# Attention scores of head pairs: plain rounded parts on 64 rows each instead of stacked parts on 128

## The chip, the cores and the metric

One core of a Trainium2 chip runs the whole network in one launch. The metric is device time in microseconds (us), the median of several executions.

## The reference, cut to what matters

Four layers work on x of 512 tokens by 1024 channels in float32. Layers 0 and 3 mix with differential attention (A), layer 1 with latent attention (B), layer 2 with dilated attention (C); each is followed by a SwiGLU block. What the change touches are the scores of A and of the undilated group of C, whose heads are all 64 channels wide:

```python
# A, layers 0 and 3: 8 pairs of heads; a pair shares its values
q = apply_rope(q, cos, sin) * 64 ** -0.5
k = apply_rope(k, cos, sin)
p = softmax(einsum('bhqd,bhkd->bhqk', q, k))          # 16 heads, 512 x 512 each
a = p[:, :, 0] - lam * p[:, :, 1]                     # the two heads of a pair
o = rms_norm(a @ v, subln) * (1.0 - lambda_init)
# C, layer 2: 16 heads, three groups (window, dilation); group 0 is (128, 1)
q = apply_rope(q, cos, sin) * 64 ** -0.5
s = where(abs(qpos - kpos) <= 64, q @ k.T, -1e30)     # group 0: a band of keys
```

## The kernel before, in words

Every float32 product that needs accuracy is made of numbers rounded to the fast matmul type: x = hi + lo, where ACT rounds (`act` with an F32R output) and DVE or POOL subtracts (`tt` with `subtract`). A projection is three products into one PSUM bank: hi·hi, hi·lo, lo·hi (`mm3`, `project`, lines 604 to 614).

The program is first written down as a list of operations with an estimated cost, an engine, and the buffers that they read and write (`Plan.op`). `Plan.run` (line 401) then schedules that list several times with changing priorities, keeps the plan with the shortest estimate, and issues the instructions in that plan's order. So the order on every engine hangs on the estimated costs of all operations; each operation stays whole, and its matmuls follow one another. PSUM has 8 banks. Buffers come from rings: a new tile waits until the tile that had its slot is no longer used.

**A** (`layer_a`, line 998). For each of 8 head pairs `rope` (line 1017) projects 128 channels of q, then of k; the upper and the lower 64 partitions of the result belong to the two heads of the pair. DVE multiplies by the cosine table and shuffles, POOL multiplies by the sine table and adds. The tables `cs` were multiplied at the start by 1/rms of each token (line 1012). `qk` (line 1046) splits: for each head s, tile `qa[s]` holds the rounded q in the head's own 64 partitions and the rest of q in the other 64; `ka[s]` holds the rounded k twice; `kl` holds the rest of k. That is 6 ACT and 4 POOL instructions on 64 partitions for each pair, in 5 tiles of a ring of 10.

For each of the 4 query tiles (line 1068) a score tile is one operation of four matmuls with 512 columns (line 1073): for each head one product over all 128 rows of the array (hi·hi and lo·hi together, as the parts are stacked), then for each head one product on its 64 rows (hi·lo). Each head's scores fill a bank, out of a ring of four. Then DVE takes the negative maximum of each head (`negmax`, line 1076), scales the two maxima by 1/8 (`ts`, line 1078, which appears at L354 in the profile), ACT takes the exponentials with scale 1/8, that bias and a row sum (line 1082), DVE inverts each of the two sums (`recip`, lines 1085 and 1087, L364), combines, and PE turns the result with four transposes (L293). The probabilities live in a ring of 5 tiles.

**C** (`layer_c`, line 1350). For each of 8 head pairs and each of three groups, `rope` (line 1372) makes q and k. For group 0 `split` (line 1384) does what `qk` does, out of a ring of 5. The scores of two query tiles, each against 256 keys, are one operation of eight matmuls (lines 1457 to 1467): for each query tile two on 128 rows, then two on 64 rows. Groups 1 and 2 multiply unsplit float32 q and k, head by head on 64 rows (line 1473): four query tiles of 128 keys in one operation. The later products with the values use all rows and half the columns of the array (`halves`, line 265, L271).

All matmuls of `mm` appear at L261, activations at L317, `tt` at L330, `stt` at L341, `negmax` at L368, the shuffle at L385.

Of the kernel before, what the change touches and what calls it, by code (L numbers as in the profile page):

```python
# [7 lines left out]
F32 = mybir.dt.float32  # L8
# [6 lines left out]
T = 512  # L15
# [163 lines left out]
class Plan:  # L179
# [85 lines left out]
    def halves(self, *parts):  # L265

        nc = self.nc

        def fn():
            for out, l, r, s, e in parts:  # L270
                nc.tensor.matmul(out.ap(), l.ap(), r.ap(), start=s, stop=e)  # L271

        cost = sum(p[2].n / 0.6 + 60.0 for p in parts[::2])
        return self.op("pe", cost, fn, _uniq([v for p in parts for v in p[1:3]]), _uniq([p[0] for p in parts]), lag=340.0)

    def tiled(self, *parts):
# [236 lines left out]
def _uniq(views):  # L513
    out, seen = [], set()
    for v in views:
        k = (id(v.buf), v.p0, v.p1, tuple(v.free))
        if k not in seen:
            seen.add(k)
            out.append(v)
    return out  # L520
# [26 lines left out]
class Net:  # L547
# [450 lines left out]
    def layer_a(self, i, j):  # L998
# [4 lines left out]
        pr, sr, tr = (Ring(p, b) for b in (self.bank[0:2], self.bank[2:6], self.bank[6:8]))  # L1003
        small = list(self.small)
        take = lambda n: Ring(p, [small.pop(0) for _ in range(n)])
        o_ring, v_ring, qk_ring, p_ring = take(16), take(8), take(10), take(5)
        aT_h, aT_l = Ring(p, self.big[0:1]), Ring(p, self.big[1:2])
        self.tables("c_rope_a")
        r = self.norm(tr)
        cs = self.rt  # L1010
        for c in range(2):
            p.tt(cs[:, c, :], cs[:, c, :], self.rb.all, ALU.mult)
        swap = [(d + 8) % 16 if d < 16 else d for d in range(32)]
        sub = self.kept.new([128, 1])
        p.ts(sub.all, self.gcol(self.rows["a_subln"] + j), 1.0 - init, ALU.mult)
# [1 line left out]
        def rope(c0):  # L1017
            ps = self.project(pr, self.wblock(w, 0, KT, c0, 128), KT, self.xk)
            q, t = self.tmp.new([128, T]), self.tmp.new([128, T])
            p.tt(q.all, ps.all, cs[:, 0, :], ALU.mult)  # L1020
            p.shuffle(t.all, ps.all, swap)
            p.tt(t.all, t.all, cs[:, 1, :], ALU.mult, eng="pool")
            p.tt(q.all, q.all, t.all, ALU.add, eng="pool")
            return q
# [20 lines left out]

        def qk(h):

            q = rope(128 * h)
            qa = [qk_ring.new([128, T], F32R) for _ in range(2)]
            for s, (a, b) in enumerate(HALVES):  # L1050
                p.act(qa[s][a, :], q[a, :])
                p.tt(qa[s][b, :], q[a, :], qa[s][a, :].bits(F32), ALU.subtract, eng="pool")
            k = rope(D + 128 * h)
            ka = [qk_ring.new([128, T], F32R) for _ in range(2)]
            kl = qk_ring.new([128, T], F32R)
            for s, (a, b) in enumerate(HALVES):
                p.act(ka[s][a, :], k[a, :])
                p.act(ka[s][b, :], k[a, :])
                p.tt(kl[a, :], k[a, :], ka[s][a, :].bits(F32), ALU.subtract, eng="pool")
            return qa, ka, kl  # L1060

        oh = []
        nxt = qk(0)
        for h in range(A_HEADS):
            qa, ka, kl = nxt
            th, tl = aT_h.new([128, NT, T], F32R), aT_l.new([128, NT, T], F32R)
            l0 = self.cols2.new([128, NT])
            for t in range(NT):
                st = self.cols.new([128, 6])
                es = [self.psum(sr) for _ in range(2)]  # L1070
                tq = slice(128 * t, 128 * (t + 1))

                p.mm(*[(es[s].all, qa[s][:, tq], ka[s].all, True, False) for s in range(2)],
                     *[(es[s].all, qa[s][HALVES[s][0], tq], kl[HALVES[s][0], :], False, True) for s in range(2)])
                for s in range(2):
                    p.negmax(st[:, s:s + 1], es[s].all)
                sc = self.cols.new([128, 2])
                p.ts(sc.all, st[:, 0:2], A_HD ** -0.5, ALU.mult)
                pe = []
                for s in range(2):  # L1080
                    e = p_ring.new([128, T])
                    p.act(e.all, es[s].all, ACTF.Exp, scale=A_HD ** -0.5, bias=sc[:, s:s + 1], accum=st[:, 2 + s:3 + s])
                    pe.append(e)

                p.recip(l0[:, t:t + 1], st[:, 2:3])
                rl = self.cols.new([128, 1])
                p.recip(rl.all, st[:, 3:4])
                p.stt(rl.all, rl.all, self.lam[:, j:j + 1], st[:, 2:3], ALU.mult, ALU.mult)
                a = pe[0]
                p.stt(a.all, pe[1].all, rl.all, pe[0].all, ALU.mult, ALU.add)  # L1090
                ps = self.psum(tr, (128, NT, 128))
                p.transposes(*[(ps[:, c, :], a[:, 128 * c:128 * (c + 1)], self.ident.all) for c in range(NT)])
                b = slice(128 * t, 128 * (t + 1))
                p.act(th[:, :, b], ps.all)
                p.tt(tl[:, :, b], ps.all, th[:, :, b].bits(F32), ALU.subtract)
            if h + 1 < A_HEADS:
                nxt = qk(h + 1)
            if h % 2 == 0:
                vv = values(h // 2)
            ps = self.psum(tr)  # L1100
            hd = slice(128 * (h % 2), 128 * (h % 2) + 128)
            for c in range(NT):
                self.mm3(ps.all, vv[0][c // 2][:, c % 2, hd], vv[1][c // 2][:, c % 2, hd], th[:, c, :], tl[:, c, :], c == 0, c == NT - 1)
            o, sq = self.tmp.new([128, T]), self.tmp.new([128, T])
            p.act(o.all, ps.all)
            p.act(sq.all, ps.all, ACTF.Square)
            s = self.colsum(tr, self.tokens(sq, False))
            v = self.cols.new([128, NT])
            p.tt(v.all, s, l0.all, ALU.mult)
            p.tt(v.all, v.all, l0.all, ALU.mult)  # L1110
            p.ts(v.all, v.all, 0.5 / A_HD, ALU.mult, EPS, ALU.add)
            ro = self.rpow(v.all, NT)
            p.tt(ro.all, ro.all, l0.all, ALU.mult)
            bc = self.spread(tr, ro)
            p.stt(o.all, o.all, sub.all, bc.all, ALU.mult, ALU.mult)
            hh, hl = o_ring.new([128, T], F32R), o_ring.new([128, T], F32R)
            p.act(hh.all, o.all)
            p.tt(hl.all, o.all, hh.all.bits(F32), ALU.subtract)
            oh.append((hh.all, hl.all))
# [230 lines left out]
    def layer_c(self, i, j):  # L1350
# [30 lines left out]
                p.tt(tiles(q.all), perm(a.all), perm(t.all), ALU.add)  # L1381
            return q

        def split(q, k):

            new = lambda: f_ring.new([128, T], F32R)
            qa, ka, kl = [new(), new()], [new(), new()], new()
            for s, (a, b) in enumerate(HALVES):
                p.act(qa[s][a, :], q[a, :])
                p.tt(qa[s][b, :], q[a, :], qa[s][a, :].bits(F32), ALU.subtract, eng="pool")  # L1390
                p.act(ka[s][a, :], k[a, :])
                p.act(ka[s][b, :], k[a, :])
                p.tt(kl[a, :], k[a, :], ka[s][a, :].bits(F32), ALU.subtract, eng="pool")
            return qa, ka, kl

        def values(g, v):

# [40 lines left out]
        for n in range(C_HEADS // 2):  # L1438
            P = {}
            sn, sp = st_ring.new([128, G, NT, 4]), st_ring.new([128, G, NT, 4])  # L1440
            for g in range(G):
                q, k = rope(3 * D * g + 128 * n, g), rope(3 * D * g + D + 128 * n, g)
                st = sn if g == 0 else sp
                if g == 0:
                    qa, ka, kl = split(q, k)

                hb = (slice(0, 64), slice(64, 128))
                if g == 0:
                    for t0 in (0, 2):
                        ps = [self.psum(sr, (128, 2, 256)) for _ in range(2)]  # L1450
                        e = 0 if t0 == 0 else 448
                        mms, spans = [], ([], [])
                        for h in range(2):
                            P[g, h, t0] = pieces[0]
                            pieces.append(pieces.pop(0))
                            p.memset(P[g, h, t0](e, e + 64), 0.0)
                        for t in (t0, t0 + 1):

                            lo = min(max(0, 128 * t - 64), T - 256)
                            d = lo - (128 * t - 64)  # L1460
                            c = slice(max(0, d), min(256, 256 + d))
                            tk, ks, o = slice(128 * t, 128 * (t + 1)), slice(lo, lo + 256), 256 * (t - t0)
                            mms += [(ps[h][:, t - t0, :], qa[h][:, tk], ka[h][:, ks], True, False) for h in range(2)]
                            mms += [(ps[h][:, t - t0, :], qa[h][hb[h], tk], kl[hb[h], ks], False, True) for h in range(2)]
                            for h in range(2):
                                spans[h].append((t, ps[h][:, t - t0, c.start - d:c.stop - d], c, P[g, h, t0](o + c.start, o + c.stop)))
                        p.mm(*mms)
                        for h in range(2):
                            self.exps(spans[h], st, g, h, scale)
                else:  # L1470
# [162 lines left out]
```

## Time and profile before

| what | us |
|---|---|
| median of 3 executions (2767.26 to 2769.59) | 2769.24 |
| the profiled execution | 2773.31 |
| its span, first to last instruction | 2771.5 |
| PE busy in the span | 2728.5 |
| DVE / ACT / POOL busy in the span | 2016.8 / 1442.2 / 699.9 |
| mean granted TensorE clock, share of full | 0.994 |

The profile shows one execution with every instruction's start and duration. PE are matmuls, PEld the weight loads that precede them and run beside the matmul before. A matmul's recorded duration has a modelled end and overlaps the next one, so what one costs is read from start to start. In the shapes, `64*128` is an array use of 64 rows and 128 columns, `128x512` the moving operand; a row that ends in x8 merges eight instructions.

### The profile page before, as it was taken

How to read it: one execution, taken by the hardware profiler on the slowest of the kernel's cores; microseconds unless marked ns; L12 is line 12 of the kernel's file. 1: busy time of each engine (PE TensorE's matmuls, PEld its weight loads, DVE VectorE, ACT ScalarE, POOL GpSimd, SP SyncE). 2: the span in 40 equal slices, each digit the busy share in tenths (PEclk: the TensorE clock that was granted, in tenths of full speed). 3: DMA queues.
4: the chain of work that ended last, by engine and by line, in shares of the span. 5: the costliest groups of instructions: out<-in, count | busy, mean ns of one | idle time of the engine just before them, and what ended most of it. 6: DMA issues, size and time to landing. Idle time of an engine off the chain costs nothing.

```text
span 2771.5 us, 43850 instructions
## 1 busy us (share of the span) xinstructions
PE 2728.5 (98%) x16565; PEld 2330.3 (84%) x16565; DVE 2016.8 (73%) x3727; ACT 1442.2 (52%) x2673; POOL 699.9 (25%) x510
## 2 busy tenths in 40 slices
PE   8999999999999999999999999999999999999999
PEld 6777899997777899988888888789998777789998
DVE  6786888766665887765758575688776688688774
ACT  5564544445874544445555555454444566454442
POOL 3343211003642210021413222221002444221101
PEclk9999999999999999999999999999999999999999
DMA  5211343323122343232222322333323211324322
GB/s 142 61 46 54 103 126 100 111 77 72 35 62 80 88 118 104 84 109 78 70 78 70 85 67 80 96 88 116 106 81 110 61 46 55 94 81 121 101 79 66
DMA packets 474977, 235.80 MB, mean 85 GB/s; under 512 B 47935, under 2 KB 471694, under 8 KB 474766
## 3 DMA queue, kind: packets, MB, share of 16 engines
q1 hardware_dynamic: 474766, 233.00, 29.8%
q8 instruction: 130, 2.13, 0.3%
q14 instruction: 81, 0.66, 0.1%
HBM read 230.66 MB, written 2.29 MB: 84 GB/s over the span
## 4 chain that ended last, share of the span: by engine, by line
PE 93%; DVE 3%; ACT 1%; DMA 1%; issue 1%; POOL 0%; SPq 0%; POOLq 0%; DVEq 0%; ACTq 0%
PE b L261 87%; PE b L293 4%; PE b L271 2%; ACT s L317 1%; DVE s L330 0%; DVE col L368 0%; PE b L282 0%; POOL tmp L330 0%; DVE wlo L330 0%; DVE tmp L330 0%; DVE tmp L385 0%; DVE s L341 0%; DMA raw<-in_a_w_qkv 0%; DVE tmp L341 0%; DVE raw L330 0%
## 5 line engine op out<-in xcount | busy, mean ns | idle before, releaser
L261 PE MATMUL b<-s,whi 128*128 128x256 f32 (+1 forms) x4000 | 867.0, 312 | 3.6 <-ACT s L317 1.4
L261 PEld LDWEIGHTS b<-s,whi 128*128 128x128 f32 x4000 | 654.7, 188 | 63.5 <-DVE tmp L330 2.3
L261 PE MATMUL b<-s,wlo 128*128 128x256 f32 (+1 forms) x2000 | 622.5, 311 | 0.8 <-DVE wlo L330 0.8
L317 ACT ACTIVATE whi<-raw 128x1024 fp32r<-128x1024 f32 (+4 forms) x350 | 367.7, 1055 | 340.6 <-PE b L261 226.2
L330 DVE TENSOR_TENSOR wlo<-raw,whi 128x1024 fp32r<-128x1024 f32 (+2 forms) x330 | 445.4, 1356 | 68.3 <-ACT whi L317 66.2
L261 PE MATMUL b<-xh,whi 128*128 128x512 f32 x1072 | 434.6, 405 | 8.6 <-DVE tmp L385 4.4
L261 PE MATMUL b<-xh,wlo 128*128 128x512 f32 x1072 | 420.6, 392 | 0.0
L261 PE MATMUL b<-xl,whi 128*128 128x512 f32 x1072 | 420.0, 392 | 0.0
L261 PEld LDWEIGHTS b<-s,wlo 128*128 128x128 f32 x2000 | 376.2, 188 | 25.6 <-DVE wlo L330 1.4
L330 DVE TENSOR_TENSOR tmp<-b,tmp 128x256 f32<-128x256 f32 (+1 forms) x297 | 128.2, 432 | 238.9 <-PE b L261 202.7
L317 ACT ACTIVATE tmp<-b 128x256 f32<-128x256 f32 (+2 forms) x301 | 126.6, 430 | 334.7 <-PE b L261 280.3
L261 PEld LDWEIGHTS b<-xh,whi 128*128 128x128 f32 x1072 | 202.4, 189 | 59.7 <-issue 8.7
L261 PEld LDWEIGHTS b<-xh,wlo 128*128 128x128 f32 x1072 | 202.3, 189 | 44.1
L330 POOL TENSOR_TENSOR tmp<-tmp,rt 128x512 f32<-128x512 f32 x83 | 116.5, 1406 | 468.5 <-DVE tmp L385 399.5
L261 PEld LDWEIGHTS b<-xl,whi 128*128 128x128 f32 x1072 | 202.9, 189 | 37.3
L261 PE MATMUL b<-s,g 128*128 128x256 f32 x1728 | 224.8, 281 | 0.0
L261 PEld LDWEIGHTS b<-s,g 128*128 128x128 f32 x1728 | 218.0, 189 | 5.9
L317 ACT ACTIVATE s<-tmp 128x512 fp32r<-128x512 f32 (+3 forms) x232 | 140.5, 613 | 90.8 <-DVE tmp L341 40.0
L330 POOL TENSOR_TENSOR acc<-acc,tmp 128x512 f32<-128x512 f32 (+1 forms) x56 | 92.9, 1659 | 355.6 <-ACT tmp L317 355.1
L261 PE MATMUL b<-xh,s 128*128 128x512 f32 x512 | 177.0, 395 | 0.0
L330 POOL TENSOR_TENSOR raw<-raw 128x512 f32<-128x512 f32 x36 | 56.5, 1569 | 434.4 <-DVE g L330 355.8
L330 POOL TENSOR_TENSOR raw<-rt,rb 128x512 f32<-128x512 f32 x36 | 58.2, 1617 | 388.9 <-DVE wlo L330 354.1
(184 smaller groups left out, 4864.9 us busy)
## 6 DMA issues: line engine op xcount, KB each, us to landing
raw<-in_f_w_gu SPq DMA_DIRECT2D x144, 256.0 KB, 3.4
raw<-in_c_w_qkv SPq DMA_DIRECT2D x72, 512.0 KB, 3.8
s<-in_f_w_out SPq DMA_DIRECT2D x128, 256.0 KB, 2.9
raw<-in_a_w_qkv SPq DMA_DIRECT2D x48, 512.0 KB, 3.7
rt<-in_f_w_gu SPq DMA_DIRECT2D x72, 256.0 KB, 3.4
raw<-in_f_w_gu SPq DMA_DIRECT2D x32, 512.0 KB, 4.8
raw<-in_f_w_out SPq DMA_DIRECT2D x32, 384.0 KB, 3.5
acc<-in_f_w_gu SPq DMA_DIRECT2D x36, 256.0 KB, 3.2
```

Of the source, the lines that this page charges most:

```text
L261: nc.tensor.matmul(out.ap(), l.ap(), r.ap(), start=s, stop=e, skip_group_check=more)
L271: nc.tensor.matmul(out.ap(), l.ap(), r.ap(), start=s, stop=e)
L293: nc.tensor.transpose(out.ap(), i.ap(), idn.ap())
L317: nc.scalar.activation(out.ap(), in_.ap(), func, **k)
L330: o = self.op(eng, cost, lambda: e.tensor_tensor(out=out.ap(), in0=a.ap(), in1=b.ap(), op=alu), [a, b], [out])
```

## The change

A head's q and k keep their own 64 partitions: `hi` is the rounded tile of both heads, `lo` the rest. Both `qk` and `split` now need one ACT and one POOL instruction on 128 partitions for q, and the same for k. A score tile becomes six products on 64 rows, in the order hi·hi of head 0, of head 1, lo·hi of both, hi·lo of both, through a new helper `pairs` with a cost of its own for the planner; in C twelve products for two query tiles. The scale 1/8 of A goes, as its square root, into the tables of q and k alike, so that the scaling of the maxima falls away; the two inversions become one on two columns. In A the ring of q and k tiles goes from 10 to 8, that of the probabilities from 5 to 7.

```diff
+    def pairs(self, *parts):
+        nc = self.nc
+        def fn():
+            for out, l, r, s, e in parts:
+                nc.tensor.matmul(out.ap(), l.ap(), r.ap(), start=s, stop=e)
+        cost = sum(0.4414 * p[2].n + 12.0 for p in parts[::2]) + 200.0
+        return self.op("pe", cost, fn, ...)
...
-        o_ring, v_ring, qk_ring, p_ring = take(16), take(8), take(10), take(5)
+        o_ring, v_ring, qk_ring, p_ring = take(16), take(8), take(8), take(7)
...
-            p.tt(cs[:, c, :], cs[:, c, :], self.rb.all, ALU.mult)
+            p.stt(cs[:, c, :], cs[:, c, :], A_HD ** -0.25, self.rb.all, ALU.mult, ALU.mult)
...
-            q = rope(128 * h)
-            qa = [qk_ring.new([128, T], F32R) for _ in range(2)]
-            for s, (a, b) in enumerate(HALVES):
-                p.act(qa[s][a, :], q[a, :])
-                p.tt(qa[s][b, :], q[a, :], qa[s][a, :].bits(F32), ALU.subtract, eng="pool")
-            k = rope(D + 128 * h)
-            ka = [qk_ring.new([128, T], F32R) for _ in range(2)]
-            kl = qk_ring.new([128, T], F32R)
-            for s, (a, b) in enumerate(HALVES):
-                p.act(ka[s][a, :], k[a, :])
-                p.act(ka[s][b, :], k[a, :])
-                p.tt(kl[a, :], k[a, :], ka[s][a, :].bits(F32), ALU.subtract, eng="pool")
-            return qa, ka, kl
+            out = []
+            for c0 in (0, D):
+                x = rope(c0 + 128 * h)
+                hi, lo = (qk_ring.new([128, T], F32R) for _ in range(2))
+                p.act(hi.all, x.all)
+                p.tt(lo.all, x.all, hi.all.bits(F32), ALU.subtract, eng="pool")
+                out += [hi, lo]
+            return out
...
-                p.mm(*[(es[s].all, qa[s][:, tq], ka[s].all, True, False) for s in range(2)],
-                     *[(es[s].all, qa[s][HALVES[s][0], tq], kl[HALVES[s][0], :], False, True) for s in range(2)])
+                p.pairs(*[(es[s].all, a[HALVES[s][0], tq], b[HALVES[s][0], :], n == 0, n == 2)
+                          for n, (a, b) in enumerate(((qh, kh), (ql, kh), (qh, kl))) for s in range(2)])
                 for s in range(2):
                     p.negmax(st[:, s:s + 1], es[s].all)
-                sc = self.cols.new([128, 2])
-                p.ts(sc.all, st[:, 0:2], A_HD ** -0.5, ALU.mult)
...
-                    p.act(e.all, es[s].all, ACTF.Exp, scale=A_HD ** -0.5, bias=sc[:, s:s + 1], accum=st[:, 2 + s:3 + s])
+                    p.act(e.all, es[s].all, ACTF.Exp, bias=st[:, s:s + 1], accum=st[:, 2 + s:3 + s])
...
-                p.recip(l0[:, t:t + 1], st[:, 2:3])
+                p.recip(ls[:, :, t], st[:, 2:4])
                 rl = self.cols.new([128, 1])
-                p.recip(rl.all, st[:, 3:4])
-                p.stt(rl.all, rl.all, self.lam[:, j:j + 1], st[:, 2:3], ALU.mult, ALU.mult)
+                p.stt(rl.all, ls[:, 1, t:t + 1], self.lam[:, j:j + 1], st[:, 2:3], ALU.mult, ALU.mult)
...
-                            mms += [(ps[h][:, t - t0, :], qa[h][:, tk], ka[h][:, ks], True, False) for h in range(2)]
-                            mms += [(ps[h][:, t - t0, :], qa[h][hb[h], tk], kl[hb[h], ks], False, True) for h in range(2)]
+                            mms += [(ps[h][:, t - t0, :], a[hb[h], tk], b[hb[h], ks], n == 0, n == 2)
+                                    for n, (a, b) in enumerate(((qh, kh), (ql, kh), (qh, kl))) for h in range(2)]
...
-                        p.mm(*mms)
+                        p.pairs(*mms)
```

`split` of C becomes the same loop as in `qk` above, out of its own ring of 5.

## Rows read from the trace of the kernel before

**Rows 1.** The page, parts 1 and 4: busy time by engine; shares of the chain.

```profile
PE 2728.5 (98%) x16565; PEld 2330.3 (84%) x16565; DVE 2016.8 (73%) x3727; ACT 1442.2 (52%) x2673; POOL 699.9 (25%) x510
...
PE 93%; DVE 3%; ACT 1%; DMA 1%; issue 1%; POOL 0%; SPq 0%; POOLq 0%; DVEq 0%; ACTq 0%
```

**Rows 2.** Stretches (start:end, length, busy by engine with counts, clock, DMA): attention A, C, A.

```profile
33.00:256.00 223.00, 214.78 (x1181) 169.08 (x1182) 176.25 (x371) 131.77 (x266) 102.11 (x71) 0.97 0.20 60
...
1236.00:1755.00 519.00, 517.44 (x3143) 430.18 (x3141) 349.53 (x1065) 278.47 (x711) 149.21 (x97) 1.00 0.28 76
...
2145.00:2370.00 225.00, 214.46 (x1179) 168.74 (x1178) 178.22 (x373) 134.51 (x269) 101.53 (x71) 0.97 0.20 59
```

**Rows 3.** Timeline, PE then PEld: the first two score tiles in a row of A.

```profile
47.01 2.14 PE L261 MATMUL b<-s,s 128*128 128x512 f32 x8
49.08 0.39 PE L261 MATMUL b<-whi,xh 128*128 128x256 f32 x1
...
46.90 0.30 PEld L261 LDWEIGHTS b<-s,s 128*128 128x128 f32 x2
47.56 0.18 PEld L261 LDWEIGHTS b<-s,s 64*128 64x128 f32 x2 [0.36 <-POOL tmp L330]
47.99 0.30 PEld L261 LDWEIGHTS b<-s,s 128*128 128x128 f32 x2 [0.24 <-issue]
48.65 0.18 PEld L261 LDWEIGHTS b<-s,s 64*128 64x128 f32 x2 [0.37 <-issue]
```

**Rows 4.** Timeline, PE: one score tile of A by itself, and what stands beside it.

```profile
77.91 0.62 PE L261 MATMUL b<-g,s 128*128 128x512 f32 x2
78.37 1.05 PE L261 MATMUL b<-s,s 128*128 128x512 f32 x4
79.36 0.50 PE L261 MATMUL b<-xh,whi 128*128 128x512 f32 x1
```

**Rows 5.** Timeline, PE: the last two score tiles in a row.

```profile
2354.23 2.15 PE L261 MATMUL b<-s,s 128*128 128x512 f32 x8
```

**Rows 6.** Timeline, PE then PEld: products on 64 rows of a dilated group, C.

```profile
1261.64 1.16 PE L261 MATMUL b<-s,s 64*128 64x128 f32 x16
...
1261.64 0.97 PEld L261 LDWEIGHTS b<-s,s 64*128 64x128 f32 x16 [0.35 <-issue]
1262.73 0.19 PEld L261 LDWEIGHTS b<-xh,whi 128*128 128x128 f32 x1
```

**Rows 7.** Timeline, PE: score blocks of C, after a projection and after half-column products.

```profile
1253.72 1.45 PE L261 MATMUL b<-s,s 128*128 128x256 f32 x8
1255.10 0.50 PE L261 MATMUL b<-xh,whi 128*128 128x512 f32 x1
...
1386.90 1.57 PE L261 MATMUL b<-s,s 128*128 128x256 f32 x8
1388.40 0.39 PE L261 MATMUL b<-whi,xh 128*128 128x256 f32 x1
```

**Rows 8.** Waits of PE in the first A stretch, then in the second.

```profile
PE b L293 <- DVE col L354: 1.9, 2, 1.6
...
PE b L261 <- DVE col L364: 1.3, 1, 1.3
...
PE b L261 <- DVE col L354: 1.1, 1, 1.1
PE b L261 <- DVE col L364: 1.1, 1, 1.1
```

**Rows 9.** Groups by line and shape, whole span: count, busy us, mean ns, idle before.

```profile
L317 ACT ACTIVATE s<-tmp 64x512 fp32r<-64x512 f32 x96 | 60.5, 630 | 34.6 <-POOL tmp L330 32.9
...
L330 POOL TENSOR_TENSOR s<-tmp,s 64x512 fp32r<-64x512 f32 x64 | 93.4, 1459 | 43.4 <-ACT s L317 39.6 <-PE b L293 1.3
...
L354 DVE TENSOR_SCALAR col<-col 128x2 f32<-128x2 f32 x64 | 24.6, 385 | 0.0
...
L364 DVE RECIPROCAL col<-col 128x1 f32<-128x1 f32 x128 | 19.5, 155 | 24.8 <-ACT s L317 24.6
```

More of the change, by code (lines that the diff above doesn't have):

```diff
@@ L273, in halves @@
         cost = sum(p[2].n / 0.6 + 60.0 for p in parts[::2])
+        return self.op("pe", cost, fn, _uniq([v for p in parts for v in p[1:3]]), _uniq([p[0] for p in parts]), lag=340.0)
+    def pairs(self, *parts):
[4 more added lines that the diff above has]
+        cost = sum(0.4414 * p[2].n + 12.0 for p in parts[::2]) + 200.0
         return self.op("pe", cost, fn, _uniq([v for p in parts for v in p[1:3]]), _uniq([p[0] for p in parts]), lag=340.0)
@@ L1064, in layer_a @@
         for h in range(A_HEADS):
-            qa, ka, kl = nxt
+            qh, ql, kh, kl = nxt
             th, tl = aT_h.new([128, NT, T], F32R), aT_l.new([128, NT, T], F32R)
-            l0 = self.cols2.new([128, NT])
+            ls = self.cols2.new([128, 2, NT])
+            l0 = ls[:, 0, :]
             for t in range(NT):
-                st = self.cols.new([128, 6])
+                st = self.cols.new([128, 4])
                 es = [self.psum(sr) for _ in range(2)]
                 tq = slice(128 * t, 128 * (t + 1))
-                p.mm(*[(es[s].all, qa[s][:, tq], ka[s].all, True, False) for s in range(2)],
-                     *[(es[s].all, qa[s][HALVES[s][0], tq], kl[HALVES[s][0], :], False, True) for s in range(2)])
+                p.pairs(*[(es[s].all, a[HALVES[s][0], tq], b[HALVES[s][0], :], n == 0, n == 2)
+                          for n, (a, b) in enumerate(((qh, kh), (ql, kh), (qh, kl))) for s in range(2)])
                 for s in range(2):
                     p.negmax(st[:, s:s + 1], es[s].all)
-                sc = self.cols.new([128, 2])
-                p.ts(sc.all, st[:, 0:2], A_HD ** -0.5, ALU.mult)
                 pe = []
@@ L1108, in layer_a @@
             v = self.cols.new([128, NT])
-            p.tt(v.all, s, l0.all, ALU.mult)
-            p.tt(v.all, v.all, l0.all, ALU.mult)
+            p.tt(v.all, s, l0, ALU.mult)
+            p.tt(v.all, v.all, l0, ALU.mult)
             p.ts(v.all, v.all, 0.5 / A_HD, ALU.mult, EPS, ALU.add)
             ro = self.rpow(v.all, NT)
-            p.tt(ro.all, ro.all, l0.all, ALU.mult)
+            p.tt(ro.all, ro.all, l0, ALU.mult)
             bc = self.spread(tr, ro)
@@ L1382, in rope, with split @@
             return q
[L1384 to L1394, printed above, removed]
+        def split(*qk):
+            out = []
+            for x in qk:
+                hi, lo = (f_ring.new([128, T], F32R) for _ in range(2))
+                p.act(hi.all, x.all)
+                p.tt(lo.all, x.all, hi.all.bits(F32), ALU.subtract, eng="pool")
+                out += [hi, lo]
+            return out
         def values(g, v):
@@ L1444, in layer_c @@
                 if g == 0:
-                    qa, ka, kl = split(q, k)
+                    qh, ql, kh, kl = split(q, k)
                 hb = (slice(0, 64), slice(64, 128))
```

## The prediction

> **What bounds the kernel now.** I read the page first, for the engine that the end hangs on. PE is busy for 2728.5 of 2771.5 us and carries 93% of the chain [rows 1]; DVE, at 2016.8, has 750 us of slack. So work taken off ACT, POOL or DVE pays only where PE waits for it. The windows by stretch say where that is [rows 2]: in C PE is idle for 519 − 517.4 = 1.6 us, in the two A stretches for 223 − 214.8 = 8.2 and 225 − 214.5 = 10.5 us. In A the mean granted clock is also 0.97 (the two levels are 2.4 and 1.2 GHz, so a few us at the lower one); if all of that went, 3% of 223 and of 225 us, 6.7 each, would come back. C is therefore bound by PE's own work, A by PE with some 19 us of waits and at most 13 us of lost clock.
>
> The third view is the timeline of the score tiles, which shows what they cost PE from start to start. A fast product of 512 columns on all rows takes (78.37 − 77.91) / 2 = 0.23 us [rows 4]. A single tile of A takes 79.36 − 78.37 = 0.99 us, two in a row 49.08 − 47.01 = 2.07 us [rows 3, 4]. That is more than three steps of 0.23, and the weight loads tell why [rows 3]. From the two loads on 64 rows to the next load on 128 rows (47.56 to 47.99, 48.65 to 49.08) pass 0.43 us: the two 64-row products run side by side, as one step of 0.23, and 0.20 goes to the change of shape. The load after such a change isn't hidden: the two 128-row loads that follow take 0.30 together and one is 0.19, so the second starts 0.11 after the first. From 47.99 to 48.65 are 0.66 = 0.11 + 2 × 0.23 + 0.09, and that 0.09 is the wait before the array goes to 64 rows. Check on the single tile: 2 × 0.23 + 0.09 + 0.43 = 0.98 against 0.99.
>
> **The score products of A.** The old tile has two steps on 128 rows and one on 64; the new one has three on 64. The number of 0.23 us steps stays at three, and only changes of shape can be saved. A tile between other work changes shape twice before and after: 0.09 + 0.43 + 2 × 0.23 = 0.98 against 0.99, so 0.01 saved. A second tile behind a first changes nothing any more: 0.09 + 0.43 + 5 × 0.23 = 1.67 against 2.07, so 0.40 saved. The code has 64 tiles (8 pairs, 4 query tiles, 2 layers); in the timeline 14 places hold two in a row, the first at 47.01, the last at 2354.23 [rows 3, 5], and 36 are single. That gives 14 × 0.40 + 36 × 0.01 = **6.0 us**. The planner may place them differently, between no place (0.6) and all 32 (13); I keep 14, because its cost of a tile hardly moves (4 × (0.4414 × 512 + 6.5) = 930 ns before, 3 × (0.4414 × 512 + 12) + 200 = 914 after).
>
> This rests on weight loads staying hidden while one 64-row step follows another with the same rows. The old score tiles never do that, but the dilated groups of C do [rows 6]: sixteen products of 128 columns, eight steps, take 1262.73 − 1261.64 = 1.09 us. Without the 0.20 of the change of shape that is 0.11 a step, the length of one load alone, so the loads run back to back and the products beside them. For 512 columns the product of 0.23 is then the longer.
>
> **The score products of C.** There a block holds two query tiles with 256 columns; I take half of 0.23, 0.12, for a step. The lone pair costs 0.12 + 0.20 = 0.32. A block behind a projection takes 1255.10 − 1253.72 = 1.38 us now, with three changes of shape inside it [rows 7]; after, 0.09 + 0.32 + 5 × 0.12 = 1.01, saving 0.37. One behind the half-column products takes 1388.40 − 1386.90 = 1.50 and comes to 0.32 + 0.60 = 0.92, saving 0.58. There are 16 blocks, 3 of the second kind; the 3 that follow transposes I price as the first. 13 × 0.37 + 3 × 0.58 = **6.5 us**. As PE has 1.6 us of idle time in all of C [rows 2], this should arrive whole.
>
> **The other engines.** In A the rounding goes from 96 ACT instructions of 0.63 us to 32, and from 64 POOL instructions of 1.46 us to 32, of the same length since only partitions are added: 40 us of ACT and 47 us of POOL less over two layers [rows 9]. DVE loses 64 scalings of 0.385 (24.6 us) and 64 of 128 inversions of 0.155 (9.9 us), together 17 us a layer out of 176 to 178 busy. The same rounding in C lies beside PE and counts as nothing; were PE not the bound there, it would be a gain too. The two table multiplications of each layer become a form with a scalar, at nothing: two DVE instructions once a layer. The smaller q and k ring holds two head pairs as before (8 tiles at 4, not 10 at 5), so it adds no wait; the larger one for probabilities lets ACT run further ahead. No DMA is moved on SP, and POOL's queue only gets shorter.
>
> What this is worth is the least certain term. It lies between 0 and all of A's idle time and lost clock, 8.2 + 10.5 + 13.4 = 32 us; a loss is possible too, as the order of every engine is drawn anew (the same program has 8.2 us of idle time in one A layer and 10.5 in the other). I take the waits that end on the removed scaling and on the inversions: 1.9 + 1.3 in the first A stretch, 1.1 + 1.1 in the second [rows 8], **5.4 us**. That is near the low end, since behind the scaling and its wait the exponential or the shuffle is late next.
>
> **Sum.** 6.0 + 6.5 + 5.4 = 17.9 us. The profiled execution took 2773.3 (its span of 2771.5 and 1.8 around it), 4.1 above the median of 2769.2. So 2773.3 − 17.9 = 2755.4 for such an execution, and **2751.3** at the median's level.
>
> **The rivals.** *A gives its share back.* Each tile's scores are followed by DVE and ACT work, DVE is busy for 79% of the A stretch, and faster PE meets the same waits sooner. Then only C's 6.5 remains: 2762.7. Against it: DVE loses 17 us a layer, PE 3. *A's waits mostly go.* The path from scores to exponential loses an instruction, and the clock stays up: with three quarters of the 32 us, 12.5 + 24 = 36.5, so 2732.7. Against it: waits behind the shuffle and the exponential have other causes that stay. *Weight loads are exposed (slower).* In a run of 64-row steps, each step's load waits until the step before with the same rows is done, at 0.11 us. Then a single tile costs 0.98 + 0.22 = 1.20 (+0.21), two in a row 1.67 + 0.55 = 2.22 (+0.15), a block of C 1.01 + 0.55 = 1.56 (+0.18) or 1.47 (−0.03): 7.6 + 2.1 + 2.3 − 0.1 = +11.9 us, and with A's 5.4 kept 2775.7. It decides from the point where a later step loses 17.9 / 222 = 0.08 us (36 × 2 + 30 × 5 = 222 later steps). Rows 6 speak against it, with steps of 0.11 in all; for it is only that no 512-column run of that kind stands in the trace.
>
> The Trainium skill states this rule, in "TensorE: Matmul & The Clock Gate", Part 3, "The mechanism": weight loads overlap with matmuls in flight only where the row groups differ. By that rule the time would be the last rival's 2775.7; the trace disagrees, with 0.11 us a step over the same rows [rows 6].
>
> *The new order costs what the products save.* New waits of 13 to 18 us in A, about as much again as stand there now: 2764 to 2769. Nothing in the rows asks for it.
>
> **How the numbers follow.** No change within 0.2% means within 5.5 us, about what a measurement can tell: 2763.7 to 2774.8. Forecast (2743 to 2759) 0.56; A gives back (2759 to 2766) 0.20; waits go (2724 to 2743) 0.12; loads exposed 0.06; new order 0.06. Faster takes the first, the third and four fifths of the second, 0.84; slower the exposed loads and a hundredth for a worse order, 0.07; no change the rest, 0.09. The range runs from 2736, which takes in the better half of the placements and part of the vanishing waits, to 2766, where A has given all back; about 0.16 lies outside.
>
> **What would show it.** Two tiles in a row should take about 1.67 us and a single one 0.98; the weight loads inside a run should start 0.23 (A) and 0.12 (C) apart, with no gap. Blocks of C should take 1.0 us, and the C stretch be 6 to 7 us shorter. In A the two-column scaling is gone from L354, 64 inversions remain for its tiles, and PE's idle time falls from 19 to 13 us or so. I am wrong if later steps are 0.34 apart, if fewer tiles stand in a row, or if A's idle time grows.

## The result, and the profile after

The changed kernel takes 2735.18 us, the median of 4 executions (2734.72 to 2736.15); beside them the kernel before took 2769.41. The ratio is 0.9875 [0.9858, 0.9892]: 34.2 us less, about twice the 17.9 of the forecast and 0.8 us below its range. The profiled executions took 2734.72 and 2773.31, so that pair shows 38.6; as the prediction said, before's lies 4 above its median. Before's time follows the clock that an execution is granted: of its 54 executions in the later comparisons, those at a mean of 0.997 took 2766.3 to 2768.8, those at 0.994 2772.7 to 2773.9, and its median lay between 2768.2 and 2772.8. So differences of 2 or 3 us between kernels of different comparisons tell nothing.

The page after, parts 1 and 4, as in [rows 1]:

```profile
PE 2703.6 (99%) x16757; PEld 2317.9 (85%) x16757; DVE 1983.2 (73%) x3599; ACT 1381.6 (51%) x2577; POOL 620.4 (23%) x462
...
PE 96%; DVE 2%; DMA 1%; ACT 1%; issue 0%; POOL 0%; SPq 0%; POOLq 0%; DVEq 0%; ACTq 0%
```

The stretches of A, C and A after, with the columns of [rows 2]:

```profile
33.00:235.00 202.00, 198.47 (x1211) 159.81 (x1210) 161.43 (x312) 111.31 (x236) 78.15 (x54) 0.99 0.23 69
...
1220.00:1731.00 511.00, 510.12 (x3201) 425.21 (x3200) 339.27 (x1065) 257.54 (x677) 119.03 (x81) 1.00 0.29 77
...
2123.00:2335.00 212.00, 207.49 (x1253) 166.49 (x1254) 167.97 (x316) 115.75 (x243) 77.74 (x55) 0.99 0.21 62
```

PE's idle time in A was 8.2 + 10.5 us [rows 2]; it is 3.5 + 4.5 now, so 10.7 less. The granted clock rises from 0.97 to 0.99 of the upper level, 2.4 GHz: what lay below full speed was 3% of 448 us, 13.4, and is 1% of 414, 4.1.

For every kernel below I also read three lengths from the timeline of PE, between the feed-forward blocks, whose products with the tile g mark their starts and ends: from the start to the first block (A 1), from the second to the third (C), from the third to the fourth (A 2). The blocks themselves take 247 to 248 us in every kernel.

```
us                                     median    A 1     C      A 2
before                                 2769.4   362.7  657.9   378.1
after                                  2735.2   347.3  650.8   363.0
products alone, before's order         2768.4   363.5  650.9   379.4
scaling gone alone, before's order     2771.3   363.2  658.2   376.9
all of the change, before's order      2753.0   357.8  650.7   369.8
rounding back, after's order           2748.8   354.4  651.0   368.9
scaling back, after's order            2735.9   348.0  651.3   363.1
```

So C gives 7.1 us, and the two stretches with A 15.4 + 15.1 in the profiled pair; at the level of the medians some 34.2 − 7.1 = 27.

The score products after, PE, then the weight loads beside the first of them, then two blocks of C:

```profile
42.51 1.65 PE L282 MATMUL b<-s,s 64*128 64x512 f32 x12
44.09 0.38 PE L261 MATMUL b<-whi,xh 128*128 128x256 f32 x1
...
46.80 0.96 PE L282 MATMUL b<-s,s 64*128 64x512 f32 x6
47.69 0.38 PE L261 MATMUL b<-whi,xh 128*128 128x256 f32 x1
...
42.51 1.22 PEld L282 LDWEIGHTS b<-s,s 64*128 64x128 f32 x12
44.09 0.19 PEld L261 LDWEIGHTS b<-whi,xh 128*128 128x128 f32 x1 [0.36 <-issue]
...
1237.37 0.98 PE L282 MATMUL b<-s,s 64*128 64x256 f32 x12
1238.27 0.50 PE L261 MATMUL b<-xh,whi 128*128 128x512 f32 x1
...
1368.36 0.97 PE L282 MATMUL b<-s,s 64*128 64x256 f32 x12
1369.26 0.39 PE L261 MATMUL b<-whi,xh 128*128 128x256 f32 x1
```

Two tiles in a row take 44.09 − 42.51 = 1.58 us, one 0.89, a block of C 0.90; with the 0.09 ahead of the change of shape 1.67, 0.98 and 0.99, against 1.67, 0.98 and 1.01 as worked out. Twelve loads take 1.22 within 1.58, with no gap: they stay hidden while one 64-row step follows another on the same rows. The Trainium skill ("TensorE: Matmul & The Clock Gate", Part 3, "The mechanism") has weight loads overlap with matmuls in flight only where the row groups differ; this trace disagrees, with (1.58 − 0.20) / 6 = 0.23 us a step on the same rows.

### The profile page after: what moved, and what is told of

It is laid out like the page before. It is cut to its first block, busy times and chain, and to the rows that moved or that the text cites. A ratio compares the mean times of both kernels' runs of the same rounds, so it can differ in the third digit from the quotient of the medians.

```text
span 2732.9 us, 43805 instructions
## 1 busy us (share of the span) xinstructions
PE 2703.6 (99%) x16757; PEld 2317.9 (85%) x16757; DVE 1983.2 (73%) x3599; ACT 1381.6 (51%) x2577; POOL 620.4 (23%) x462
## 4 chain that ended last, share of the span: by engine, by line
PE 96%; DVE 2%; DMA 1%; ACT 1%; issue 0%; POOL 0%; SPq 0%; POOLq 0%; DVEq 0%; ACTq 0%
PE b L261 87%; PE b L304 4%; PE b L282 2%; PE b L271 2%; PE b L293 0%; ACT s L328 0%; DVE tmp L341 0%; DMA raw<-in_a_w_qkv 0%; DVE s L341 0%; DVE raw L341 0%; DVE wlo L341 0%; DVE tmp L396 0%; DMA rb<-in_f_w_gu 0%; ACT tmp L328 0%; DMA s<-in_x 0%
## 5 line engine op out<-in xcount | busy, mean ns | idle before, releaser
L328 ACT ACTIVATE whi<-raw 128x1024 fp32r<-128x1024 f32 (+4 forms) x350 | 367.1, 1054 | 337.3 <-PE b L261 226.9
L341 DVE TENSOR_TENSOR wlo<-raw,whi 128x1024 fp32r<-128x1024 f32 (+2 forms) x330 | 446.4, 1360 | 73.1 <-ACT whi L328 71.0
L341 DVE TENSOR_TENSOR tmp<-b,tmp 128x256 f32<-128x256 f32 (+1 forms) x297 | 127.9, 431 | 239.7 <-PE b L261 202.2
L328 ACT ACTIVATE tmp<-b 128x256 f32<-128x256 f32 (+2 forms) x301 | 126.1, 429 | 330.3 <-PE b L261 278.5
L341 POOL TENSOR_TENSOR tmp<-tmp,rt 128x512 f32<-128x512 f32 x83 | 118.8, 1433 | 491.9 <-DVE tmp L396 457.1
L341 POOL TENSOR_TENSOR acc<-acc,tmp 128x512 f32<-128x512 f32 (+1 forms) x56 | 93.1, 1662 | 361.0 <-ACT tmp L328 360.6
L341 POOL TENSOR_TENSOR raw<-raw 128x512 f32<-128x512 f32 x36 | 56.5, 1568 | 437.1 <-DVE g L341 379.8
L379 DVE TENSOR_REDUCE col<-b 128x1 f32<-128x512 f32 x192 | 126.6, 684 | 36.8 <-PE b L261 21.1
L328 ACT ACTIVATE s<-b,col 128x512 f32<-128x512 f32 x196 | 133.1, 686 | 34.5 <-DVE col L379 22.7
```

Of the source, the lines that this page charges most:

```text
L328: nc.scalar.activation(out.ap(), in_.ap(), func, **k)
L341: o = self.op(eng, cost, lambda: e.tensor_tensor(out=out.ap(), in0=a.ap(), in1=b.ap(), op=alu), [a, b], [out])
L379: return self.op("dve", (a.n + 148) / 0.96, lambda: nc.vector.tensor_reduce(out=out.ap(), in_=a.ap(), op=ALU.max, axis=AX, negate=True), [ ...
```

## The experiments

Two theories for what the forecast lacks. **The work**: the lighter rounding and the scaling shorten what PE waits for in A, beyond the waits that bear their names. **The order**: the schedule is drawn anew, and the new one is better. Many kernels therefore keep an order: the operation stays in the list with its cost and its place, and only what it issues is replaced ("in before's order", with before's rings, or "in after's order"). Where rounding is put back in after's tiles, the second rounding of each half of k is only repeated; no kernel leaves out part of the result. The expectations call some kernels by number: e3 has the scaling back and e5 the rounding back, each with a schedule of its own; e8 is before without the scaling, e9 has the rounding back in after's order, e16 is after with two score tiles in one operation.

**All of the change in before's order**: every operation of `qk`, `split` and the tile keeps its place; of a group the first ACT operation and the last POOL operation issue the whole instruction, the others nothing.

```diff
+                p.emit(o, [(es[s].all, a[HALVES[s][0], tq], b[HALVES[s][0], :], n == 0, n == 2)
+                           for n, (a, b) in enumerate(((qa[0], ka[0]), (qa[1], ka[0]), (qa[0], kl))) for s in range(2)])
-                p.ts(sc.all, st[:, 0:2], A_HD ** -0.5, ALU.mult)
+                p.ts(sc.all, st[:, 0:2], A_HD ** -0.5, ALU.mult).fn = lambda: None
```

> All instructions of the changed kernel, but issued in the order that was planned for the kernel before (same buffers and rings as before; the scaling, the second inversion and the spare rounding instructions are simply left out of it). Theory 'work': the waits of PE in A go because DVE, ACT and POOL have less to do; then nearly the whole gain is here, 2735 to 2742 us, and both A layers have under 10 us of PE waits. Rival 'order': the waits went because the planner drew a new order; then only the products' 12 us and a little more are here, 2752 to 2758 us, with A's waits at the old places.

2752.99 us, 0.9934 [0.9919, 0.9949]. The work without the new order is worth 16.4 us (17.2 in its own comparison); the other 17.8 come with the order and the rings.

**The products alone in before's order**: six 64-row products, but as many roundings as before, and the scaling.

> The score products alone: six 64-row products a tile, with as many rounding instructions on 64 partitions as before, the scaling and both inversions kept, and the order of the kernel before on every engine. My sum for the products says 12.5 us less, 2757 us. Theory 'work' expects that and A's waits unchanged at about 19 us; if the shorter tiles themselves free the waits, it is under 2748 us.

```diff
-                p.act(qa[s][a, :], q[a, :])
+                p.act(qa[s][a, :], q[a, :]).fn = lambda o=qa[0][a, :], x=q[a, :]: self.nc.scalar.activation(o.ap(), x.ap(), ACTF.Copy)
```

2768.38, 0.9993 [0.9983, 1.0002]: 1.0 us by the medians. The profiled executions, both at a clock of 0.994, differ by 4.5: C is 7.0 us shorter, and the two stretches with A are 2.1 longer, although PE has some 6 us less to do there. The rest goes with the clock: all ten executions of this kernel had 0.994 or 0.995, before's 0.995 to 0.997 beside them. Its windows of A, then the waits of PE in the first and second A stretch (L1070 rounds k, L327 the other activations, L303 the transposes, L364 the scaling), and before's waits for ACT in the same stretches:

```profile
33.00:256.00 223.00, 212.45 (x1239) 168.61 (x1240) 176.62 (x372) 130.52 (x265) 101.02 (x71) 0.97 0.22 62
...
2138.00:2364.00 226.00, 213.09 (x1243) 169.66 (x1242) 181.46 (x372) 133.82 (x268) 99.86 (x71) 0.97 0.20 59
```
```profile
PE b L271 <- ACT s L1070: 2.2, 2, 1.4
PE b L303 <- DVE col L364: 1.9, 2, 1.6
...
PE b L271 <- ACT s L1070: 3.4, 2, 2.5
PE b L271 <- ACT s L327: 1.6, 2, 1.4
```
```profile
PE b L261 <- ACT s L317: 1.7, 4, 1.1
...
PE b L261 <- ACT s L317: 2.9, 4, 1.7
```

Idle time is 10.6 + 12.9, more than before's 8.2 + 10.5. The score products already waited for ACT before, 1.7 and 2.9; now it is 2.4 and 5.0, of which the rounding of k has 2.2 and 3.4. That is the first rival, *A gives its share back*, as long as the work around the products stays.

**The scaling gone alone in before's order**: of the edits of the first kernel only those of the tables, the scaling, the exponential and the inversions.

```diff
-                p.recip(l0[:, t:t + 1], st[:, 2:3])
+                p.recip(ls[:, 0, t:t + 1], st[:, 2:3]).fn = lambda: None
-                p.recip(rl.all, st[:, 3:4])
+                p.recip(rl.all, st[:, 3:4]).fn = lambda o=ls[:, :, t], x=st[:, 2:4]: self.nc.vector.reciprocal(out=o.ap(), in_=x.ap())
```

> The kernel before in its own order on every engine, without the scaling and with one inversion on two columns; products and rounding as before. My prediction's term says 5.4 us less, 2764. If the waits behind these instructions only pass to the next one in the queue: 2767 to 2771. e8 with a new order had 9 less.

2771.26, 1.0004 [0.9995, 1.0013]: worth nothing. The waits of PE in the first and in the second A stretch:

```profile
PE b L322 <- DVE s L370: 3.5, 4, 1.6
PE b L261 <- DVE tmp L414: 2.1, 2, 1.8
...
PE b L261 <- DVE tmp L414: 4.7, 3, 2.4
PE b L322 <- DVE s L370: 3.1, 4, 1.5
```

The rows that named the scaling [rows 8] are gone, one of 1.3 us still names the inversion that is left (L1120), and PE waits as long as before: the waits that the two views name are 12.2 + 10.4 us before and 12.5 + 10.1 here. The timelines show that rows 8 were misread. Two of those waits before, then the first of them here:

```profile
112.98 0.75 DVE L341 SCALAR_TENSOR_TENSOR s<-s,col,s 128x512 f32<-128x512 f32 x1
113.64 0.16 DVE L354 TENSOR_SCALAR col<-col 128x2 f32<-128x2 f32 x1
113.87 0.63 PE L293 MATMUL b<-ident,s 128*128 128x128 f32 x4 [1.60 <-DVE col L354]
...
114.98 0.73 DVE L385 STREAM_SHUFFLE tmp<-b 128x512 f32<-128x512 f32 x1
115.60 0.14 DVE L364 RECIPROCAL col<-col 128x1 f32<-128x1 f32 x1
115.76 0.58 PE L261 MATMUL b<-whi,xh 128*128 128x256 f32 x1 [1.26 <-DVE col L364]
```
```profile
112.45 0.75 DVE L370 SCALAR_TENSOR_TENSOR s<-s,col,s 128x512 f32<-128x512 f32 x1
...
113.35 0.63 PE L322 MATMUL b<-ident,s 128*128 128x128 f32 x4 [1.59 <-DVE s L370]
```

The transposes turn what the combination of the two heads (L341, here L370) writes. They start 0.14 us after its end with the scaling, which belongs to another tile, in between, and 0.15 after it without. The projection needs a bank that the shuffle reads, and starts 0.05 after the shuffle's end. Every wait that rows 8 put down to the scaling or an inversion comes behind a combination or a shuffle in this way: the row names what ended last on DVE, not what PE needed.

**The scaling and two inversions back, in after's order.** Each maximum is scaled by itself (128 small DVE instructions).

```diff
+                    o.fn = lambda real=o.fn, ...: (real(), self.nc.vector.tensor_scalar(
+                        out=o.ap(), in0=x.ap(), scalar1=A_HD ** -0.5, ...))
```

> The changed kernel in its own order, with the scaling done again (one column at a time, directly behind each maximum, so 128 small DVE instructions where the kernel before had 64) and two inversions instead of one. My prediction's term (waits of PE behind these instructions, 5.4 us) says 2740 us or more. If they cost nothing since the rounding is gone: 2735 to 2737.

2735.9, 0.9875 [0.986, 0.989], 0.7 above after: nothing, in this order too.

**The rounding back in after's order**, in halves of 64 partitions, both engines, then POOL alone, then ACT alone:

```diff
-                p.act(hi.all, x.all)
-                p.tt(lo.all, x.all, hi.all.bits(F32), ALU.subtract, eng="pool")
+                o, u = p.act(hi.all, x.all), p.tt(lo.all, x.all, hi.all.bits(F32), ALU.subtract, eng="pool")
+                o.fn = lambda ...: [self.nc.scalar.activation(hi[a, :].ap(), x[a, :].ap(), ACTF.Copy)
+                                    for a in (slice(0, 64), slice(64, 128)) for _ in range(n)]
+                u.fn = lambda ...: [self.nc.gpsimd.tensor_tensor(out=lo[a, :].ap(), ...) for a in (slice(0, 64), slice(64, 128))]
```

> The changed kernel with its own order on every engine, but A's rounding issued as six ACT and four POOL instructions on 64 partitions for a head pair, at the places of the whole ones. Theory 'work': the extra 20 us of ACT and 23 us of POOL a layer bring A's waits back: 2750 us or more, as with the order drawn anew (2754). Rival 'order': the changed order takes them without waits: 2735 to 2741.

2748.8, 0.9919 [0.9904, 0.9933]: 13.6 us of the gain gone.

> As e9, but only the POOL instructions doubled (four of 64 partitions instead of two of 128). If POOL's work is what matters (its own latency, and the longer DVE instructions beside it), most of e9's loss is here, and the 512-column combination on DVE takes over 0.9 us in the mean again (0.78 in the changed kernel). If ACT's, 2735 to 2738.

2741.99, 0.9893 [0.9879, 0.9908]: POOL alone, 6.8.

> As e9, but only the ACT instructions multiplied (six of 64 partitions instead of two of 128). If ACT's work is what matters, most of e9's loss is here; if POOL's, 2735 to 2738.

2740.06, 0.9885 [0.9869, 0.9902]: ACT alone, 4.9. The same comes out in before's order: from the products alone to all of the change are 2768.4 − 2753.0 = 15.4, and the scaling that lies between them is worth nothing there; part of it comes through the clock, 0.994 or 0.995 in the former and 0.996 to 0.998 in the latter.

Groups by line (count, busy us, mean ns, idle before) after, before, with POOL's part back and with ACT's part back:

```profile
L352 DVE SCALAR_TENSOR_TENSOR s<-s,col,s 128x512 f32<-128x512 f32 x64 | 49.8, 779 | 0.4
...
L341 POOL TENSOR_TENSOR s<-tmp,s 128x512 fp32r<-128x512 f32 x32 | 48.9, 1528 | 22.9 <-ACT s L328 22.9
```
```profile
L341 DVE SCALAR_TENSOR_TENSOR s<-s,col,s 128x512 f32<-128x512 f32 x64 | 58.0, 907 | 0.0
```
```profile
L352 DVE SCALAR_TENSOR_TENSOR s<-s,col,s 128x512 f32<-128x512 f32 x64 | 59.4, 930 | 0.4
...
L1065 POOL TENSOR_TENSOR s<-tmp,s 64x512 fp32r<-64x512 f32 x64 | 91.8, 1435 | 21.0 <-ACT s L328 18.6
```
```profile
L352 DVE SCALAR_TENSOR_TENSOR s<-s,col,s 128x512 f32<-128x512 f32 x64 | 50.6, 791 | 0.4
...
L1065 ACT ACTIVATE s<-tmp 64x512 fp32r<-64x512 f32 x96 | 60.4, 629 | 19.7 <-POOL tmp L341 18.0
```

POOL's rounding lengthens DVE's combination, the work that PE's transposes wait for: 779 ns after, 930 with POOL's instructions back, 791 with ACT's (876 with both). That is one way from POOL to PE; the rounding's own wait, seen above, is another.

**The rounding back, schedule drawn for it**, and then **after's work in that schedule**:

```diff
-                p.act(hi.all, x.all)
-                p.tt(lo.all, x.all, hi.all.bits(F32), ALU.subtract, eng="pool")
+                for a in (slice(0, 64), slice(64, 128)):
+                    for _ in range(2 if c0 else 1):
+                        p.act(hi[a, :], x[a, :])
+                    p.tt(lo[a, :], x[a, :], hi[a, :].bits(F32), ALU.subtract, eng="pool")
```

> The changed kernel with A's rounding done as often as before: six ACT and four POOL instructions on 64 partitions for a head pair (two of the ACT ones repeat another). If ACT's and POOL's relief frees A's waits, 2745 us or more; if DVE's does, 2735 to 2739 us. My prediction priced it at nothing.

2754.39, 0.9932 [0.9918, 0.9947]: 19.2 above after, where each of the two works has a schedule of its own.

> The work of the changed kernel in the order planned for rounding in halves (that of e5, 2754 us). Theory 'work': 2735 to 2742, since nothing but work differs. Rival 'order': the order planned for more ACT and POOL work holds the waits: 2748 us or more.

2745.35, 0.9906 [0.9891, 0.9921]. The lighter rounding is worth 9.0 in this order. Either work runs slower in it than in after's: by 5.6 and by 10.2.

**The scaling back, schedule drawn for it**, and then the same work drawn again with 0.1 more in the planner's cost of a product:

```diff
-                p.recip(ls[:, :, t], st[:, 2:4])
+                p.recip(ls[:, 0, t:t + 1], st[:, 2:3])
+                p.recip(ls[:, 1, t:t + 1], st[:, 3:4])
+                p.ts(sc.all, st[:, 0:2], A_HD ** -0.5, ALU.mult)
```

> The changed kernel with the scaling of the two maxima and the two separate inversions put back (35 us of DVE over both A layers), order drawn anew. If DVE's relief is what frees A's waits, most of the 19 us beyond the products comes back: 2748 us or more. If it is the rounding on ACT and POOL, 2735 to 2740 us. My prediction's term for it was 5.4 us, 2740.5 us.

2732.28, 0.9855 [0.9838, 0.9871], no slower than after.

```diff
-            cost += (0.4414 * n + 6.5) if fast else ...
+            cost += (0.4414 * n + 6.6) if fast else ...
```

> The changed kernel with scaling and two inversions back (e3, 2732 us), with 0.1 ns added to the planned cost of a fast matmul, so only the order differs. If e3's lead over the changed kernel is a draw of the order: 2735 us or more. If doing without the scaling is a loss in itself: 2730 to 2734 again.

2746.14, 0.9913 [0.9896, 0.9929]. The same instructions in another drawing cost 13.9 us more. Not all of that is in A: layer B, between the first two feed-forward blocks, is the same work in every kernel and takes 336.5 to 337.1 us where the cost is 6.5, but 339.2 to 341.0 in the four kernels with 6.6. The stretches of the two profiled executions:

```
us                                      A 1      B      C    A 2
scaling back, schedule drawn for it   346.5  336.7  650.8  357.5
the same, drawn again                 351.0  340.7  651.5  364.4
```

**Before and after, drawn again** by the same edit:

> The kernel before with 0.1 ns added to the planned cost of a fast matmul: no instruction changes, the order is drawn anew. Theory 'work': within 4 us of before, 2765 to 2773. Rival 'order': a new order alone moves A's waits by 10 us or more, so 2759 or less, or 2779 or more, can come out.

2770.48, 1.0001 [0.9992, 1.0011], 0.3 from before in its comparison; in the profiled pair A is 5.8 us shorter and B 2.5 longer.

> The changed kernel with 0.1 ns added to the planned cost of a fast matmul (the pairs keep theirs): no instruction changes, the order is drawn anew. Theory 'work': 2731 to 2740 us. Rival 'order': the low waits of A were a lucky draw, and a new one gives 2745 us or more.

2738.07, 0.9884 [0.9869, 0.9899], 2.9 above after, 2.7 of them in B.

**Before with the scaling gone, drawn anew** (the change's own lines for the tables, the scaling, the exponential and the inversions):

> The kernel before with only the scaling folded into the tables and the two inversions merged; products on 128 rows and rounding as before, order drawn anew. If DVE's relief frees A's waits by itself, 2769 less 10 to 19 us: 2750 to 2759. My prediction's term says 5.4 us: 2764. If the rounding is what does it, 2766 to 2770.

2763.41, 0.9968 [0.9955, 0.9981]: 6.0 us less than before (9.4 in its own comparison). They are the new order's, as the same edit in the old order gave none.

**The ring of probabilities back at 5** in the kernel after:

```diff
-        o_ring, v_ring, qk_ring, p_ring = take(16), take(8), take(8), take(7)
+        o_ring, v_ring, qk_ring, p_ring = take(16), take(8), take(8), take(5)
```

> The changed kernel with 5 tiles for the probabilities as before, not 7. If the longer ring is what lets ACT run ahead and frees A's waits, 2742 us or more; by theory 'work' 2733 to 2738 us.

2735.75, 0.9865 [0.985, 0.988]: 0.6 from after, with a schedule of its own: nothing speaks for a worth of the larger ring.

**Two score tiles in one operation**, to save more changes of shape: first on the kernel with the scaling back, then on after, then drawn again.

```diff
-                p.pairs(*[(es[s].all, a[HALVES[s][0], tq], ...) ... for s in range(2)])
+                if t % 2 == 0:
+                    both = [[self.psum(sr) for _ in range(2)] for _ in range(2)]
+                    p.pairs(*[(both[u][s].all, a[HALVES[s][0], 128 * (t + u):128 * (t + u + 1)], ...)
+                              for u in range(2) for n, (a, b) in ... for s in range(2)])
+                es = both[t % 2]
```

> e3 with the scores of two query tiles in one operation, so that all 32 couples stand in a row: 19 more than in the changed kernel, 19 x 0.40 = 7.6 us less of PE's work, 2725 us, if PE still bounds A. All four score banks must then be free at once: if that wait is the bound, 2735 us or more.

2748.71, 0.992 [0.9905, 0.9936]: 16.4 worse than the kernel it was made from, but 2.6 from that kernel's second drawing.

> The changed kernel (scaling gone) with the scores of two query tiles in one operation. If PE bounds A: 2735 - 7.6 = 2728 us or less. If the wait for four free banks is the bound, 2738 us or more.

2728.36, 0.9848 [0.9834, 0.9863], 6.8 below after and the fastest of all.

> e16 (the changed kernel, two score tiles in one operation) with 0.1 ns added to the planned cost of a fast matmul. If the 7 us over the changed kernel are PE's fewer changes of shape: 2726 to 2731. If they are a draw of the order: 2735 or more.

2730.45, 0.9864 [0.9847, 0.988], still 4.7 below after, although B takes 4.2 longer than in the fastest. Windows of the fastest:

```profile
33.00:230.00 197.00, 193.99 (x1210) 159.00 (x1209) 162.75 (x310) 110.73 (x235) 78.09 (x53) 1.00 0.24 70
2110.00:2320.00 210.00, 204.99 (x1259) 168.40 (x1252) 169.11 (x314) 114.96 (x240) 76.94 (x56) 0.99 0.23 65
```

All 32 places hold two tiles there, against 13 after. 19 more at the forecast's saving, 2 × 0.98 − 1.67 = 0.29 each, are 5.5 us.

## Why the prediction was wrong

The direction was right, and so were the prices of the score products; the size in A was not.

- **Score products of A**: prices met (1.67 and 0.98), 13 places for 14, so PE has some 6 us less to do. As a gain it doesn't stand by itself: in before's order A grew by 2.1 in the profiled pair.
- **Score products of C**: 6.5 forecast, 7.1 measured, and 7.0 of it with the products alone. C has no waits to give it back to.
- **The step that failed** is the value of the other engines' relief in A, 5.4 us from "the waits that end on the removed scaling and on the inversions", with nothing for the rounding there. Both halves fell. The scaling and the inversions are worth nothing in either order: rows 8 name them because they ran last on DVE, while PE waited for the combination or the shuffle just ahead of them. The prediction expected the exponential or the shuffle to be late next and still counted the rows. The rounding, put down as 40 us of ACT and 47 of POOL and then given no place in the sum, is worth 13.6 to 15.4 in a fixed order and 19.2 where each work has its own schedule.
- **The order**: the remaining 17.8 us come with the new schedule and rings. The sum held nothing for it, and the fourth rival only a loss, of 13 to 18 us; it brought as much. The ring of probabilities adds none; the smaller ring of q and k was not tried by itself. How much of this the lighter work gives and how much is luck of the drawing stays open. For luck: one work drawn twice differed by 13.9, three other pairs by 0.3, 2.9 and 2.1. For the work: the two stretches with A take 699.6 to 721.1 us together in the eight kernels whose schedule was drawn for the whole rounding (mean 709.2) and 731.1 to 740.8 in the four drawn for it in halves (mean 734.7). After, at 710.3, is an average one of its kind, and before, at 740.8, the longest of its own. So of 30.5 us some 25 look like the work's, and 5 like before's draw and low clock; with one profile each of kernels that differ in other things too, that is a sign and no proof.
- **The bound** was sound: 32 us of idle time and lost clock in A. The change took 10.7 of the idle time and 9.3 of the clock, 20 in all; with the products' 6 that makes 26 of the 30.5 of the profiled pair. The rival that came true is *A's waits mostly go*, 2732.7, given 0.12. Its trigger, that the path loses an instruction, was not the cause: the rounding and the order were.
- *Weight loads are exposed* fell as rows 6 said: the two tiles in a row above take 0.23 us a step, with nothing left for a load.

The ladder of the medians: products −1.0, rounding with the scaling −15.4, order and rings −17.8; of the profiled executions −4.5, −15.9 and −18.2. Other sequences of the same steps could share it out in another way.

## What to carry to other kernels

A wait row names the instruction that ended last, which may be a bystander: before pricing its removal, look in the timeline for the instruction that makes or frees what the waiting engine needs. Value a relief by all the work that feeds the stretch, engines with slack included. In a kernel whose order a planner draws, measure each part in a fixed order first, and draw the whole again once or twice before trusting a gain of a few us; here such drawings differed by 0.3 to 13.9, some of it in a layer that no edit touched. Where a stretch has both waits and a lowered clock, look at both, and compare executions at the same clock: here waits and lost clock fell together.

## What the hardware showed

POOL's subtraction slows a DVE instruction that it shares no data with. The combination of 512 columns, two operands from SBUF, took 779 ns in the mean beside 32 POOL subtractions and 930 beside 64, while 64 more instructions on ACT left it at 791. Of its 64 times, 48 in after and 37 with POOL's part back overlap no POOL instruction, and each of these takes 732 to 754 ns. Every longer one overlaps a POOL instruction; those that overlap the subtraction number 3, with a mean of 1118 ns, and 12, with 1478. The longest with POOL's part back, and the two subtractions beside it:

```profile
101.17 1.87 DVE L352 SCALAR_TENSOR_TENSOR s<-s,col,s 128x512 f32<-128x512 f32 x1
...
99.82 2.66 POOL L1065 TENSOR_TENSOR s<-tmp,s 64x512 fp32r<-64x512 f32 x2
```

The Trainium skill ("SBUF — State Buffer", "Who interferes with whom") says that a VectorE instruction with two SBUF inputs and a GpSimd instruction that reads SBUF exclude each other on a shared pair of ports. The rows agree, 0.75 us alone against 1.87 in this meeting; no run here shows the ports themselves.

The subtraction itself takes about as long on 64 partitions (1435 ns) as on 128 (1528), and a rounding on ACT 629 against 628 (group L328, `s<-tmp`, in after): half the partitions save POOL 6% and ACT nothing, and the number of instructions counts.
